# A streaming encoder layer on one core: the states of its state space groups keep the rows of the turning frame, and first operands of its MLP are formed on VectorE

## The chip, the core and the metric

The kernel runs on one of the eight cores of a Trainium2 chip. Its engines work side by side, each through its own queue in order: TensorE (PE: matmuls, with weight loads as PEld), VectorE (DVE), ScalarE (ACT), GpSimd (POOL) and SyncE (SP, which here issues DMAs). They wait for each other on semaphores. The metric is the device time of one execution in microseconds (us).

## The reference

One layer over 16 meta tokens, 2048 prompt frames and 64 frames of a running stream, 2128 tokens of width 1024, all in float32. Cut to what matters here:

```python
z = rmsnorm(h, norm1_g) @ w_in                # split into q, k, v (attention) and u
q, k, v, u = split(z)                         # u: 32 groups of 16 channels
attn = sliding-window attention with sinks
bu = einsum(u, B_bar)                         # per group: 64 complex states
xs = scan(x[t] = a * x[t-1] + bu[t])          # complex, diagonal; the sample starts from h0
y  = Re(C x) + D u                            # back to 16 channels per group
zs = gelu(y); s = zs * sigmoid(zs @ w_glu + b_glu)
h  = h + concat(rmsnorm(attn), rmsnorm(s)) @ w_out
f  = rmsnorm(h, norm2_g) @ w_up               # 1024 -> 4096
return h + square(relu(f)) @ w_down, ..., xs[last] of both streams
```

## The kernel before

**Layout and stages.** Activations lie with channels on the partitions and tokens along the row. Matmuls split each float32 operand into a high part in float32r (a rounded copy made on ACT) and a low part, the rest (a subtraction on DVE or POOL, names ending in `l`), and sum three products; so each product on PE has a cast on ACT and a subtraction on DVE behind it. Some small matmuls run on plain float32: one such matmul of the program is two PE records in the profile. The stages follow each other: projection to u, projection to q, k, v with attention (to some 450 us), the state space groups together with the attention half of the output projection (to some 600 us), the GLU with the other half of that projection (to some 770 us), and the MLP.

**State space groups.** Tokens are taken in blocks of 8, 266 blocks. The 32 groups run as 16 pairs. For a pair `j`, `ssm_in` multiplies u with a table from `reca` into two PSUM banks, `pss`, one per group: the 64 real parts in rows 0 to 63, the 64 imaginary parts in rows 64 to 127. `ssm_align` (ACT, four copies of 64 rows) turns this around into `RI`: real parts of both groups in one half of the row, imaginary parts in the other, group 0 in rows 0 to 63 and group 1 in rows 64 to 127. `ssm_mix` works in this arrangement on DVE: steps 0 and 1 turn the values into a rotating frame (`o1`, `o2`, `ab`), in which the complex scan becomes two real ones (steps 2 and 3, L1272, one long call for the prompt and one of 8 columns for the sample each); step 4 multiplies back (`p1`, `p2`, L1276 and L1277), and step 5 forms the states `H` (two tiles that take turns). There, four calls of 64 rows (L1282 and L1285) put each group's states in a tile with real parts in rows 0 to 63 and imaginary parts in rows 64 to 127, two small copies keep the final states (`fin`, L1287) and put the sample's start in its place (L1288, from `h0`). `ssm_out` sums, per group, a product over u (L1294) and one over the 128 rows of states (L1295) with tables from `recb` into `psy`; `ssm_done` copies it out on ACT as `ys`, `ssm_write` stores it. `store_k` has written these tables, four pairs at a time.

**Opening of the MLP.** The MLP uses Strassen's scheme on halves of tokens, inputs and hidden units: seven products of half size instead of eight, each over sums or differences of blocks of the normed activations. `x0_load` reads blocks a, b, c of the first tokens from `hd`, where the output projection has stored them; `gain` multiplies by the weight of the norm on ACT (L1778, with `slow`) and the reciprocal root on POOL (L1782), or both on DVE (L1780); `x0_sub` (L1809) forms the differences, `x_cut` (L1790 and L1791) the high and low parts `xh`, `xl`. Block d needs the output projection's last store, so `x0_last` loads it last, in two parts `sa`, `sb`, and `x0_rest` treats it. `product(i, q)` are the matmuls (L1973) into banks bA, bB, bC. `h_squares` adds up the squares of the output projection for the norm (L1648, L1651), on POOL.

**What sets the order.** The program text is not the order. `Order.arrange` takes all instructions, a cost for each, their dependencies and buffers, runs a list schedule backward and forward, and fixes the order on each engine. So each edit can move instructions elsewhere. It knows that POOL and DVE calls that read two operands from SBUF exclude each other (`ported`). POOL calls stand in the same plan as all others.

Of the kernel before, what the change touches and what calls it, by code (L numbers as in the profile page):

```python
# [377 lines left out]
def tile_trunk(ctx: ExitStack, tc: tile.TileContext, I, O, dbg=None, stop=None):  # L378
# [60 lines left out]
    def prep(pp, pg, pgb):  # L439
# [185 lines left out]
        def store_k(q, pk):  # L625
# [3 lines left out]
            for c, t in enumerate((vr, vi)):  # L629
                for gg in range(2):  # L630
                    r = slice(64 * gg, 64 * gg + 64)
                    nc.sync.dma_start(recb[js, 64 * c : 64 * c + 64, gg * P : (gg + 1) * P].rearrange("j p (d c) -> p j d c", c=16),
                                      t[r, :, 1:9, :])
# [585 lines left out]
    def ssm_open():  # L1219
        Sx["sp"] = ssp.enter_context(pool("sp", 1, "right"))  # L1220
        h0 = Sx["h0"] = Sx["sp"].tile([P, G], F32, name="h0")
        nc.sync.dma_start(h0, I["h0"])
        Sx["fin"] = Sx["sp"].tile([P, 2, G], F32, name="fin")
# [32 lines left out]
    def ssm_mix(j, i):  # L1256
# [21 lines left out]
        elif i == 5:  # L1278
            H = x["H"] = GH[j % 2]
            for gg in range(2):  # L1280
                r = slice(64 * gg, 64 * gg + 64)
                v.tensor_sub(H[0:64, gg, 1:], x["p1"][r, 0], x["p2"][r, 1])  # L1282
            for gg in range(2):
                r = slice(64 * gg, 64 * gg + 64)
                v.tensor_add(H[64:, gg, 1:], x["p1"][r, 1], x["p2"][r, 0])  # L1285
            gs = slice(2 * j, 2 * j + 2)
            v.tensor_copy(Sx["fin"][:, :, gs].rearrange("p q g -> p g q"), H[:, :, PCH : NCH + 1 : NCH - PCH])  # L1287
            v.tensor_copy(H[:, :, PCH], Sx["h0"][:, gs])  # L1288

    def ssm_out(j):  # L1290
        x = Sx[j]
        y = x["y"] = Sx["py"]()
        for gg in range(2):
            nc.tensor.matmul(y[:, gg, :NCH], x["rb"][:, (2 + gg) * P : (3 + gg) * P], x["U"][:, gg], start=True, stop=False)  # L1294
            nc.tensor.matmul(y[:, gg, :NCH], x["rb"][:, gg * P : gg * P + P], x["H"][:, gg, 0:NCH], start=False, stop=True)  # L1295

# [329 lines left out]
    nc.sync.dma_start(O["st"], Sx["fin"])  # L1626
# [13 lines left out]
    def h_squares(n, e, x):  # L1640
# [5 lines left out]
        if e == 0:  # L1646
            HS[n] = WO["na"].tile([P, OB], F32, tag=f"hs{n}", name="hs", bufs=1)
            nc.gpsimd.tensor_add(HS[n], sq[:, 0], sq[:, 1])  # L1648
        else:
            for i in range(2):  # L1650
                nc.gpsimd.tensor_add(HS[n], HS[n], sq[:, i])  # L1651
# [121 lines left out]
    def gain(x, k0, nh, slow=False):  # L1773
# [7 lines left out]
        if slow:  # L1781
            nc.gpsimd.tensor_mul(x, x, M["rs"][:, nh].unsqueeze(1).broadcast_to((P, 2, OB)))  # L1782
# [327 lines left out]
    def rs_first(nh):  # L2110
# [6 lines left out]
    out_block(NOB - 1, {0: (lambda: x0_sub("d", "b", "a", e), lambda: u_get(0, (0, 0), (1, 0))),  # L2117
                        1: (lambda: x0_cut(1, "a", v), lambda: x0_gain("c", 1, 1), lambda: u_get(0, (1, 1), (0, 1))),
                        2: (lambda: x0_sub("b", "c", "b", e),), 3: (lambda: x0_sub("a", "c", "d", v),),
# [140 lines left out]
```

## Time and profile before

| | us |
|---|---|
| median of 3 runs (2100.11 to 2104.24) | 2102.73 |
| the profiled execution, its own time | 2103.09 |
| its span in the profile | 2100.5 |
| PE busy, 12100 matmul records | 2003.0 (95%) |
| PEld busy | 1931.1 (92%) |
| DVE busy | 1800.0 (86%) |
| ACT busy | 1221.7 (58%) |
| POOL busy | 397.0 (19%) |

The span is what the profile's rows lie in; 2.6 us of the execution's time lie around it. Busy shares are means over stages with different limits, and so say little alone. In the trace, `<-` names what ended a wait; a name such as `xl` stands for all buffers of that name, and `L1791` is the kernel's line. A row with `128x266 f32<-128x266 f32` gives rows by columns of the output and the input; `128*128` on PE gives rows and columns of the weights.

### The profile page before, as it was taken

What the parts mean: (1) busy time and instruction counts of PE and PEld (TensorE: products, weight loads), DVE (VectorE), ACT (ScalarE), POOL (GpSimd) and SP (SyncE); (2) the same over time, 40 slices, a digit from 0 to 9 for tenths busy, and PEclk for the clock granted to TensorE, in tenths of its full rate; (3) what the DMA queues carried; (4) which work ended last, traced back from release to release, by engine and by line L of the source; (5) the groups of instructions that cost most, each with busy time, mean ns of one, the idle gap of its engine ahead of it and who ended that gap; (6) DMA issues with size and microseconds to landing.
All of it is one profiled execution on the core that took longest, in us unless ns stands there. A gap on an engine that the chain in (4) does not pass through costs nothing.

```text
span 2100.5 us, 34600 instructions
## 1 busy us (share of the span) xinstructions
PE 2003.0 (95%) x12100; PEld 1931.1 (92%) x12100; DVE 1800.0 (86%) x3315; ACT 1221.7 (58%) x2496; POOL 397.0 (19%) x525
## 2 busy tenths in 40 slices
PE   8989999997789988999999999999999999999999
PEld 8987888786679977999999999999999999999999
DVE  8958996679977778999999998789978977887778
ACT  6447677743255545655555666665656655566554
POOL 7954311000002052333233301000000100000000
PEclk9999999999899998999999999999999999999999
DMA  6532332467664385654666676556745764444432
GB/s 224 153 63 76 98 97 72 146 210 239 205 209 127 118 263 189 212 181 165 226 215 201 210 249 220 160 150 207 224 140 152 240 200 141 137 135 138 138 121 96
DMA packets 308335, 354.41 MB, mean 169 GB/s; under 512 B 28865, under 2 KB 220992, under 8 KB 307650
## 3 DMA queue, kind: packets, MB, share of 16 engines
q1 hardware_dynamic: 308018, 352.21, 53.8%
q8 instruction: 95, 1.56, 0.3%
q14 instruction: 78, 0.64, 0.1%
q10 hardware_dynamic: 144, 0.00, 0.0%
HBM read 260.15 MB, written 94.07 MB: 169 GB/s over the span
## 4 chain that ended last, share of the span: by engine, by line
PE 67%; DVE 19%; ACT 5%; DMA 5%; issue 3%; SPq 0%; POOL 0%; DVEq 0%; ACTq 0%; POOLq 0%
PE psd L2068 28%; PE bB L1973 10%; PE bA L1973 10%; PE bC L1973 8%; PE pso L1454 3%; PE psqkv L920 3%; PE psg L1672 2%; DMA hd<-xo 1%; PE pu L825 1%; DVE ul L1963 1%; DVE ab L1272 1%; DVE ss L799 1%; PE pv L1185 1%; DVE wl L2037 1%; DVE acc L2077 1%
## 5 line engine op out<-in xcount | busy, mean ns | idle before, releaser
L2068 PE MATMUL psd<-hh,wh 128*128 128x352 f32 x1344 | 433.8, 323 | 3.8 <-DVE acc L2077 2.9
L2068 PE MATMUL psd<-hl,wh 128*128 128x352 f32 x1344 | 432.0, 321 | 2.0 <-DVE hl L2056 2.0
L2068 PE MATMUL psd<-hh,wl 128*128 128x352 f32 x1344 | 430.6, 321 | 0.0
L2077 DVE TENSOR_TENSOR acc<-psd,acc 128x352 f32<-128x352 f32 x624 | 313.2, 514 | 36.5 <-PE psd L2068 35.7
L2068 PEld LDWEIGHTS psd<-hh,wh 128*128 128x128 f32 x1344 | 252.0, 188 | 6.2 <-DVE acc L2077 3.8
L2068 PEld LDWEIGHTS psd<-hl,wh 128*128 128x128 f32 x1344 | 252.7, 188 | 2.7 <-DVE hl L2056 2.6
L2068 PEld LDWEIGHTS psd<-hh,wl 128*128 128x128 f32 x1344 | 252.3, 188 | 0.0
L1962 ACT CAST uh<-ur 128x512 fp32r<-128x512 f32 x144 | 89.3, 620 | 151.3 <-PE bB L1973 64.0
L2037 DVE TENSOR_TENSOR wl<-d,wh 128x512 fp32r<-128x512 f32 x240 | 175.2, 730 | 0.3 <-ACT wh L2036 0.2
L2036 ACT CAST wh<-d 128x512 fp32r<-128x512 f32 x240 | 146.5, 617 | 34.1 <-PE psd L2068 28.3
L1973 PE MATMUL bA<-xl,uh 128*128 128x352 f32 x480 | 155.9, 325 | 5.4 <-DVE xl L1791 5.4
L1973 PE MATMUL bA<-xh,uh 128*128 128x352 f32 x480 | 157.6, 328 | 3.0 <-ACT xh L1790 1.6
L1962 ACT CAST uh<-us 128x512 fp32r<-128x512 f32 x128 | 79.4, 621 | 133.5 <-PE bB L1973 68.5
L1973 PE MATMUL bB<-xh,uh 128*128 128x352 f32 x480 | 156.0, 325 | 0.0
L1973 PE MATMUL bA<-xh,ul 128*128 128x352 f32 x480 | 155.9, 325 | 0.0
L1973 PE MATMUL bB<-xh,ul 128*128 128x352 f32 x480 | 155.4, 324 | 0.0
L1973 PE MATMUL bB<-xl,uh 128*128 128x352 f32 x480 | 154.8, 323 | 0.0
L920 PE MATMUL psqkv<-wqa,xh 128*128 128x384 f32 (+1 forms) x544 | 138.3, 348 | 7.0 <-ACT z L933 6.7
L1973 PE MATMUL bC<-xl,uh 128*128 128x352 f32 x384 | 125.4, 327 | 5.6 <-DVE xl L1791 5.6
L2056 DVE TENSOR_TENSOR hl<-hid,hh 128x352 fp32r<-128x352 f32 x240 | 129.2, 538 | 1.1 <-ACT hh L2055 1.1
L1963 DVE TENSOR_TENSOR ul<-ur,uh 128x512 fp32r<-128x512 f32 x144 | 108.7, 755 | 24.6 <-ACT uh L1962 24.6
L1973 PE MATMUL bC<-xh,ul 128*128 128x352 f32 x384 | 125.2, 326 | 2.3 <-DVE ul L1963 2.2
(446 smaller groups left out, 5295.7 us busy)
## 6 DMA issues: line engine op xcount, KB each, us to landing
ur<-in_w_up_dram SPq DMA_DIRECT2D x160, 256.0 KB
d<-in_w_down_dram SPq DMA_DIRECT2D x128, 256.0 KB
us<-usd SPq DMA_DIRECT2D x128, 256.0 KB
d<-dsd SPq DMA_DIRECT2D x96, 256.0 KB
hd<-xo SPq DMA_DIRECT2D x48, 352.0 KB
usd<-s SPq DMA_DIRECT2D x64, 256.0 KB
dsd<-d SPq DMA_DIRECT2D x48, 256.0 KB
dx<-in_w_down_dram SPq DMA_DIRECT2D x48, 256.0 KB
```

The lines of the kernel that those rows point to most:

```text
L799: nc.vector.tensor_reduce(out=ss[b], in_=x.rearrange("p k n -> p n k"), axis=AX.X, op=ALU.add)
L920: nc.tensor.matmul(t["ps"][c][:n, :384], x, w[k][:, c * 384 : c * 384 + 384], start=(k == 0 and i == 0), stop=(k == KT - 1 and i == 2))
L1454: nc.tensor.matmul(ps, w, x, start=(i == 0), stop=(i == len(seq) - 1))
L1672: nc.tensor.matmul(ps, w[:, k, m * P : (m + 1) * P], x[:, k], start=(k == 0 and i == 0), stop=(k == 3 and i == 2))
L1962: nc.scalar.copy(h, src)
L1963: nc.vector.tensor_sub(l, src, f32(h))
L1973: nc.tensor.matmul(ps, w[:, k], x[:, k], start=(p in BANK and k == 0 and a == 0), stop=False, skip_group_check=True)
L2036: nc.scalar.copy(h, src)
L2037: (e if p in POOLED[i >= NPR] else v).tensor_sub(l, src, f32(h))
L2056: eng.tensor_sub(l, src, f32(h))
L2068: nc.tensor.matmul(ps, w[:, c], y, start=(p in DFIRST and n == 0), stop=False, skip_group_check=True)
L2077: v.tensor_add(ACC[eh, nh][:, x], ps, ACC[eh, nh][:, x])
```

## The change

It has two parts. In the state space groups, `H` keeps the arrangement of the rotating frame: group 0 in rows 0 to 63, group 1 in rows 64 to 127, real and imaginary parts side by side along the row. Two DVE calls of 128 rows (L1279, L1280 in the new numbering) replace the four of 64. `ssm_out` takes two products of 64 rows per group instead of one of 128 (L1298), `store_k` stores the tables accordingly, with two DMAs instead of four. The two small copies per pair go from DVE to ACT (L1281, L1282); `h0` comes from the input `par`, which has it in this arrangement, and a new function `ssm_last` turns the final states into the output's arrangement with four copies on ACT. In the other part, calls go from POOL to DVE: the sums of squares of `h_squares`, the product with the root in `gain`, two differences of `x0_sub` and the low part of `x0_cut(2, ...)`.

```diff
@@ store_k
             for c, t in enumerate((vr, vi)):
-                for gg in range(2):
-                    r = slice(64 * gg, 64 * gg + 64)
-                    nc.sync.dma_start(recb[js, 64 * c : 64 * c + 64, gg * P : (gg + 1) * P].rearrange("j p (d c) -> p j d c", c=16),
-                                      t[r, :, 1:9, :])
+                nc.sync.dma_start(recb[js, :, c * P : (c + 1) * P].rearrange("j p (d c) -> p j d c", c=16), t[:, :, 1:9, :])
@@ ssm_open
-        h0 = Sx["h0"] = Sx["sp"].tile([P, G], F32, name="h0")
-        nc.sync.dma_start(h0, I["h0"])
-        Sx["fin"] = Sx["sp"].tile([P, 2, G], F32, name="fin")
+        h0 = Sx["h0"] = Sx["sp"].tile([P, 2, PAIRS], F32, name="h0")
+        nc.sync.dma_start(h0, I["par"][:, 3:5])
+        Sx["fin"] = Sx["sp"].tile([P, 2, 2, PAIRS], F32, name="fin")
+        Sx["st"] = Sx["sp"].tile([P, 2, G], F32, name="st")
@@ ssm_mix, step 5
             H = x["H"] = GH[j % 2]
-            for gg in range(2):
-                r = slice(64 * gg, 64 * gg + 64)
-                v.tensor_sub(H[0:64, gg, 1:], x["p1"][r, 0], x["p2"][r, 1])
-            for gg in range(2):
-                r = slice(64 * gg, 64 * gg + 64)
-                v.tensor_add(H[64:, gg, 1:], x["p1"][r, 1], x["p2"][r, 0])
-            gs = slice(2 * j, 2 * j + 2)
-            v.tensor_copy(Sx["fin"][:, :, gs].rearrange("p q g -> p g q"), H[:, :, PCH : NCH + 1 : NCH - PCH])
-            v.tensor_copy(H[:, :, PCH], Sx["h0"][:, gs])
+            v.tensor_sub(H[:, 0, 1:], x["p1"][:, 0], x["p2"][:, 1])
+            v.tensor_add(H[:, 1, 1:], x["p1"][:, 1], x["p2"][:, 0])
+            nc.scalar.copy(Sx["fin"][:, :, :, j].rearrange("p q c -> p c q"), H[:, :, PCH : NCH + 1 : NCH - PCH])
+            nc.scalar.copy(H[:, :, PCH], Sx["h0"][:, :, j])
+
+    def ssm_last():
+        for c in range(2):
+            for gg in range(2):
+                nc.scalar.copy(Sx["st"][64 * c : 64 * c + 64, :, gg::2], Sx["fin"][64 * gg : 64 * gg + 64, :, c])
+        nc.sync.dma_start(O["st"], Sx["st"])
@@ ssm_out
-            nc.tensor.matmul(y[:, gg, :NCH], x["rb"][:, gg * P : gg * P + P], x["H"][:, gg, 0:NCH], start=False, stop=True)
+            r = slice(64 * gg, 64 * gg + 64)
+            for c in range(2):
+                nc.tensor.matmul(y[:, gg, :NCH], x["rb"][r, c * P : c * P + P], x["H"][r, c, 0:NCH], start=False, stop=(c == 1))
@@ after the last pair
-    nc.sync.dma_start(O["st"], Sx["fin"])
+    ssm_last()
@@ h_squares
-            nc.gpsimd.tensor_add(HS[n], sq[:, 0], sq[:, 1])
+            nc.vector.tensor_add(HS[n], sq[:, 0], sq[:, 1])
-                nc.gpsimd.tensor_add(HS[n], HS[n], sq[:, i])
+                nc.vector.tensor_add(HS[n], HS[n], sq[:, i])
@@ gain
-            nc.gpsimd.tensor_mul(x, x, M["rs"][:, nh].unsqueeze(1).broadcast_to((P, 2, OB)))
+            nc.vector.tensor_mul(x, x, M["rs"][:, nh].unsqueeze(1).broadcast_to((P, 2, OB)))
@@ the last output block, and x0_rest
-    x0_sub("d", "b", "a", e)
+    x0_sub("d", "b", "a", v)
-    x0_sub("b", "c", "b", e)
+    x0_sub("b", "c", "b", v)
-    x0_cut(2, "d", e)
+    x0_cut(2, "d", v)
```

The order of the instructions is unchanged up to some 450 us of the trace before, and again from some 1050 us on. Between them it moves at these places.

DVE in the state space stage, one pair, before: `H` with a number is one of the two state tiles, `ab` the scan's values, `xo` an addition of the output projection.

```order
L1282 TENSOR_TENSOR H_5195<-p_5885,p_5886 64x266 x2
L1285 TENSOR_TENSOR H_5195<-p_5885,p_5886 64x266 x2
L1272 SCALAR_TENSOR_TENSOR ab<-r_90,ab 128x258
L1287 COPY fin<-H_5195 128x2x2
L1272 SCALAR_TENSOR_TENSOR ab<-r_90,g_89,ab 128x8
L1288 COPY H_5195<-h_5190 128x2
L1272 SCALAR_TENSOR_TENSOR ab<-r_90,ab 128x258
L1272 SCALAR_TENSOR_TENSOR ab<-r_90,g_89,ab 128x8
L1496 TENSOR_TENSOR xo<-pso,xo 128x352 x2
```

The same place after the change:

```order
L1266 TENSOR_TENSOR ab<-o_5873,o_5874 128x266
L1270 SCALAR_TENSOR_TENSOR ab<-r_90,ab 128x258
L1270 SCALAR_TENSOR_TENSOR ab<-r_90,g_89,ab 128x8
L1279 TENSOR_TENSOR H_5188<-p_5878,p_5879 128x266
L1280 TENSOR_TENSOR H_5188<-p_5878,p_5879 128x266
L1270 SCALAR_TENSOR_TENSOR ab<-r_90,ab 128x258
L1270 SCALAR_TENSOR_TENSOR ab<-r_90,g_89,ab 128x8
L1499 TENSOR_TENSOR xo<-pso,xo 128x352 x2
```

The four calls of 64 rows have become two of 128, and stand between the scans of the next pair; the two copies are gone from this engine.

PE in the same stage, before: `psy<-U` and `psy<-H` are the products over u and over the states, `pss` the way into the states of a later pair, `pso` the output projection.

```order
L1294 MATMUL psy<-U,rb 128x266
L1295 MATMUL psy<-H_5193,rb 128x266
L1294 MATMUL psy<-U,rb 128x266
L1295 MATMUL psy<-H_5193,rb 128x266
L1245 MATMUL pss<-U,ra 128x266 x2
L1294 MATMUL psy<-U,rb 128x266
L1454 MATMUL pso<-xh,zt 128x352
```

After the change:

```order
L1295 MATMUL psy<-U,rb 128x266
L1298 MATMUL psy<-H_5186,rb 128x266 x2
L1295 MATMUL psy<-U,rb 128x266
L1298 MATMUL psy<-H_5186,rb 128x266 x2
L1243 MATMUL pss<-U,ra 128x266 x2
L1295 MATMUL psy<-U,rb 128x266
L1298 MATMUL psy<-H_5188,rb 128x266 x2
L1295 MATMUL psy<-U,rb 128x266
L1298 MATMUL psy<-H_5188,rb 128x266 x2
```

Each product over the states has become two, one behind the other; PE's other rows are the same number, 278 matmuls of the output projection in this stage in both kernels, spread differently.

DVE at the opening of the MLP, before: from the last addition of the output projection (`xo<-pso`) on; `xa` to `xd` are blocks, `sa` and `sb` the parts of the block loaded last, `xl` low parts of the products' operands, `ul` that of a weight.

```order
L1496 TENSOR_TENSOR xo<-pso,xo 128x352
L1809 TENSOR_TENSOR xa<-xc,xd 128x704
L1791 TENSOR_TENSOR xl_8176<-xd,xh_8175 128x704
L1809 TENSOR_TENSOR xa<-xc,xd 128x704
L1791 TENSOR_TENSOR xl_8106<-xa,xh_8105 128x704
L1780 SCALAR_TENSOR_TENSOR sa<-sa,g_7792,rs 128x352 x2
L1791 TENSOR_TENSOR xl_8176<-xd,xh_8175 128x704
L1791 TENSOR_TENSOR xl_8106<-xa,xh_8105 128x704
L1780 SCALAR_TENSOR_TENSOR sb<-sb,g_7792,rs 128x352 x2
L1791 TENSOR_TENSOR xl_8220<-xc,xh_8219 128x704
L1809 TENSOR_TENSOR xa<-sa,xa 128x704
L1791 TENSOR_TENSOR xl_8220<-xc,xh_8219 128x704
```

After the change, from the two last additions of the output projection on:

```order
L1966 TENSOR_TENSOR ul<-s,uh 128x512
L1499 TENSOR_TENSOR xo<-pso,xo 128x352 x2
L1794 TENSOR_TENSOR xl_8103<-xa,xh_8102 128x704 x2
L1794 TENSOR_TENSOR xl_8173<-xd,xh_8172 128x704
L1794 TENSOR_TENSOR xl_8188<-xb,xh_8187 128x704
L1794 TENSOR_TENSOR xl_8173<-xd,xh_8172 128x704
L1794 TENSOR_TENSOR xl_8217<-xc,xh_8216 128x704
L1794 TENSOR_TENSOR xl_8188<-xb,xh_8187 128x704
L1794 TENSOR_TENSOR xl_8217<-xc,xh_8216 128x704
L1966 TENSOR_TENSOR ul<-s,uh 128x512
L1783 SCALAR_TENSOR_TENSOR sa<-sa,g_7789,rs 128x352 x2
L1966 TENSOR_TENSOR ul<-ur,uh 128x512
```

All low parts of the blocks a to d stand ahead of the two products of `sa` and `sb`; before, four of the rows shown stand behind the products of `sa`, those of `xb` come later still, and POOL had the differences `xd` and `xb`. On PE the first product's twelve matmuls have moved in among the last of the output projection.

## Rows read from the trace of the kernel before

**Rows 1.** Busy time by stage: us, busy us of each engine (instructions), clock, DMA share.
```profile
458.90:594.00 135.10, 103.68 (x466) 84.59 (x465) 133.02 (x310) 43.59 (x92) 0.00 (x0) 0.91 0.72 229
...
640.00:754.00 114.00, 113.44 (x691) 111.09 (x689) 86.08 (x138) 60.56 (x101) 21.35 (x18) 1.00 0.50 153
754.00:769.00 15.00, 14.94 (x91) 14.60 (x92) 9.85 (x14) 4.62 (x8) 13.13 (x8) 1.00 0.89 292
769.00:831.00 62.00, 45.69 (x218) 40.76 (x217) 50.81 (x65) 32.44 (x62) 22.94 (x13) 0.81 0.57 190
840.00:1260.00 420.00, 414.22 (x2564) 411.01 (x2563) 412.10 (x738) 252.99 (x516) 124.69 (x71) 1.00 0.64 207
```

**Rows 2.** Groups of 458.9 to 594 us: count | busy us, mean ns | idle before.
```profile
L1295 PE MATMUL psy<-H,rb 128*128 128x266 f32 x64 | 22.7, 440 | 8.9 <-DVE H L1288 8.9
L1254 ACT COPY RI<-pss 64x266 f32<-64x266 f32 x60 | 22.5, 376 | 35.5 <-PE pss L1245 30.9 <-DVE ab L1267 4.0
...
L1245 PE MATMUL pss<-U,ra 128*128 128x266 f32 x60 | 19.4, 442 | 14.2 <-DMA ra<-reca 12.4 <-DMA U<-ud 1.7 <-issue 0.2
...
L1282 DVE TENSOR_TENSOR H<-p,p 64x266 f32<-64x266 f32 x32 | 13.6, 424 | 0.6 <-PE psy L1295 0.4
```

**Rows 3.** DVE in order of time, one pair of groups: start us, us, instruction.
```profile
502.06 0.42 DVE L1268 TENSOR_TENSOR ab<-o,o 128x266 f32<-128x266 f32 x1
502.40 0.86 DVE L1282 TENSOR_TENSOR H<-p,p 64x266 f32<-64x266 f32 x2
503.28 0.88 DVE L1285 TENSOR_TENSOR H<-p,p 64x266 f32<-64x266 f32 x2
504.19 0.70 DVE L1272 TENSOR_TENSOR_SCAN ab<-r,ab 128x258 f32<-128x258 f32 x1
504.80 0.15 DVE L1287 COPY fin<-H 128x4 f32<-128x4 f32 x1
504.86 0.23 DVE L1272 TENSOR_TENSOR_SCAN ab<-r,g,ab 128x8 f32<-128x8 f32 x1
```

**Rows 4.** PE in order of time, state space stage.
```profile
491.71 0.61 PE L1295 MATMUL psy<-H,rb 128*128 128x266 f32 x2
492.16 0.39 PE L1245 MATMUL pss<-U,ra 128*128 128x266 f32 x1
```

**Rows 5.** Groups of PE over the span, products of 64 and 81 rows.
```profile
L1185 PE MATMUL pv<-e,VB 81*128 81x256 f32 x132 | 40.4, 389 | 0.7 <-ACT e L1176 0.7
...
L1185 PE MATMUL pv<-e,VB 64*128 64x256 f32 x4 | 1.4, 428 | 0.0
```

**Rows 6.** PE's weight loads in order of time, near the 64-row product.
```profile
177.36 0.29 PEld L1185 LDWEIGHTS pv<-e,VB 64*128 64x128 f32 x2 [0.16 <-issue]
```

**Rows 7.** Groups of POOL from 640 to 786 us.
```profile
L1651 POOL TENSOR_TENSOR hs<-hs,sq 128x352 f32<-128x352 f32 x12 | 13.6, 1135 | 14.2 <-ACT sq L1645 13.7
...
L1809 POOL TENSOR_TENSOR xd<-xb,xa 128x704 f32<-128x704 f32 x2 | 4.0, 2023 | 0.0
```

**Rows 8.** DVE in order of time at the opening of the MLP.
```profile
769.21 0.51 DVE L1496 TENSOR_TENSOR xo<-pso,xo 128x352 f32<-128x352 f32 x1
...
771.54 2.35 DVE L1791 TENSOR_TENSOR xl<-xd,xh 128x704 fp32r<-128x704 f32 x1
...
774.62 0.88 DVE L1791 TENSOR_TENSOR xl<-xa,xh 128x704 fp32r<-128x704 f32 x1
775.42 1.07 DVE L1780 SCALAR_TENSOR_TENSOR sa<-sa,g,rs 128x352 f32<-128x352 f32 x2
...
780.24 1.92 DVE L1780 SCALAR_TENSOR_TENSOR sb<-sb,g,rs 128x352 f32<-128x352 f32 x2 [2.15 <-DMA d<-in_w_down_dram]
```

**Rows 9.** PE in order of time at the opening of the MLP.
```profile
783.01 0.66 PE L1973 MATMUL bC<-xl,uh 128*128 128x352 f32 x1 [2.63 <-DVE xl L1791]
...
800.81 0.66 PE L1973 MATMUL bA<-xl,uh 128*128 128x352 f32 x1 [3.31 <-DVE xl L1791]
```

More of the change, by code (lines that the diff above doesn't have):

```diff
@@ L2116, in tile_trunk @@
                         5: (lambda: rs_first(1), lambda: x0_load("c", 1, 1)), 6: (lambda: x0_gain("a", 0, 0),), 7: (lambda: x0_gain("b", 0, 1),)})
-    out_block(NOB - 1, {0: (lambda: x0_sub("d", "b", "a", e), lambda: u_get(0, (0, 0), (1, 0))),
+    out_block(NOB - 1, {0: (lambda: x0_sub("d", "b", "a", v), lambda: u_get(0, (0, 0), (1, 0))),
                         1: (lambda: x0_cut(1, "a", v), lambda: x0_gain("c", 1, 1), lambda: u_get(0, (1, 1), (0, 1))),
-                        2: (lambda: x0_sub("b", "c", "b", e),), 3: (lambda: x0_sub("a", "c", "d", v),),
+                        2: (lambda: x0_sub("b", "c", "b", v),), 3: (lambda: x0_sub("a", "c", "d", v),),
                         4: (lambda: u_sum(0, 1, 2),), 5: (lambda: x0_cut(6, "a", v),),
```

## The prediction

> **What bounds the kernel now.** I read the view by stages first: busy time of each engine, granted clock and DMA share per stretch [rows 1]. The reader is to see that the limits differ. From 640 to 754 us PE is busy 113.44 of 114 us, and from 840 to 1260 us 414.22 of 420: there PE sets the pace, at 414.22 / 2564 = 0.162 us a record. In between lie two stretches where PE is held. One is the state space stage, 458.9 to 594 us: DVE is busy 133.02 of 135.1 us, PE has 466 records. The other is the opening of the MLP, 769 to 831 us: 218 PE records in 62 us, which at 0.162 us would be 35.3 us, so 26.7 us are lost, at a mean granted clock of 0.81. After 840 us the order of the instructions is nearly the same in both kernels, and PE sets the pace, so time won in these two stretches should stay won.
>
> Next I read the costliest groups inside the state space stage [rows 2] and one pair of groups on DVE in order of time [rows 3]; then PE [rows 4, 5, 6]; last POOL, DVE and PE around the opening of the MLP [rows 7, 8, 9].
>
> **State space stage, DVE.** Before, the states of a pair are written by four calls of 64 rows, 32 calls each of L1282 and L1285, 0.424 us each [rows 2]. From start to start the four take 504.19 - 502.40 = 1.79 us [rows 3]. After, two calls of 128 rows and the same 266 columns do it. A call of that very size (L1268) stands 502.40 - 502.06 = 0.34 us before the next [rows 3]; the calls that go took 0.45. So two cost 0.68 to 0.90 us, and a pair saves 0.89 to 1.11 us; 16 pairs save 14.2 to 17.8 us. I take the lower figure, since the new calls read what was just written, as the old ones do. The two small copies per pair leave DVE too: the next call starts 504.86 - 504.80 = 0.06 us after one [rows 3], so 32 of them give 1.9 us. DVE's need falls by 16.1 us, to 135.1 - 16.1 = 119 us.
>
> **The copies on ACT.** ACT is busy 43.59 of 135.1 us in the stage [rows 1]. Before shows no ACT copy of 4 elements: one costs above nothing and below the 0.376 us of the 64x266 copy [rows 2]; I take 0.15, what the same copy lasts on DVE [rows 3]. 32 are 5 us, hidden by ACT's idle time. They add a wait: PE's product of the states now waits for ACT, whose queue also holds the copies out of PSUM (RI, ys). Behind a waiting fin copy stand the RI copies of a pair that DVE takes up about one pair later, so a wait of a microsecond or two hides there. Today the two copies stand among the scans, the first 504.80 - 504.19 = 0.61 us after the last H call gave way to a scan; two copies of 0.15 us on ACT end no later. I cost it at nothing; without that cover it is 32 times 0.15, 5 us.
>
> **The products on PE.** Before, each group takes one product of 128 rows over the states; after, two of 64 rows: 32 more. One program product is two records, and takes 492.16 - 491.71 = 0.45 us from start to start at full clock [rows 4]. No row shows a 64-row product of this kind. Below it could be near nothing, if halves ran side by side; but both halves of a group use the same rows and follow each other, so nothing suggests it. Above, the nearest pair: the 64*128 products of the attention last 428 ns against 389 ns for 81*128 [rows 5], a tenth more. I take 0.45: 14.4 us more. PE's need today at full clock: 188 fp32 records (64 over the states, 64 over U into the same sums, 60 into the states) at 0.225 us, 270 others at 0.162 and 8 of the norm sums (counted like them) give 42.3 + 45.0 = 87 us of 135.1 [rows 1, 2]; after, 102 us. The mean clock of 0.91 can add up to 0.09 x 135.1 = 12 us. That is still under DVE's 119 us, but close enough that waits of both engines on each other show. I allow 4 us: the stage then lasts 123 us, 12 us less. Bounds: 19 us less (all DVE gains, no coupling) and 3 us less (PE at 114 and each DMA wait of today's 14.2 us on PE [rows 2] also held by the denser DVE).
>
> The Trainium skill, TensorEngine Tiling (Array Packing), section Key Properties, says that a change of the tiling mode drains TensorE. Were a 64-row product such a mode, each pair would change it four times.
>
> The weight load ahead of the only 64-row product of the attention stands 0.16 us idle [rows 6]; 64 such gaps are 10.2 us, PE's need 112 us. This is a rival below.
>
> **Stores and loads.** The 64-row halves of recb are stored by two DMAs instead of four for each of four quarters, the same bytes; the load of rb is unchanged in size. h0 comes from another input with the same 16 KB. The final states take four ACT copies of 64x32 more before their store; nothing on the chain waits for that store, and ACT is idle there. Together nothing (0 to 1 us, if the last ys copy stands behind them).
>
> **Sums of squares on DVE.** 14 calls of 1.135 us leave POOL [rows 7]. On DVE a call of 704 columns takes 0.80 us [rows 8], so these of 352 cost less than 11 us in all, in a stretch where DVE is busy 86.08 of 114 us and PE full [rows 1]. PE hides it; 0 to 1 us.
>
> **The opening of the MLP.** Twelve calls of 128x704 (products with the norm, differences, two low parts) leave POOL, where one takes 2.02 us [rows 7], for DVE, where the next starts 775.42 - 774.62 = 0.80 us later [rows 8]. DVE's own calls beside them were stretched: the same low part takes 2.35 us at 771.54 and 0.88 us at 774.62 [rows 8], and POOL is busy 13.13 of the 15 us before 769 [rows 1]. So the chain of ten calls halves, and DVE as a whole is hardly fuller: 9.6 us come, some 9 us of stretch go. The order then changes in a way that matters more. Before, the low parts of xc and xb stood behind the two sb products, which waited for a load until 780.24 [rows 8]; PE stood 2.63 us at 783.01 and 3.31 us at 800.81 for them [rows 9]. After, all eight low parts stand ahead of that load, so the first product's twelve matmuls run between the output projection's, and four more products follow on. These two stalls go (5.9 us). Of the low clock, 0.19 x 62 = 11.8 us are at stake [rows 1]; I take back a quarter, 3 us, since after these products PE must still wait for the sa and sb loads, which follow the last store (769.21 to 780.24, 11 us [rows 8]). Against it, DVE must do the ten calls before its last xo additions: 8 us into a stretch with 5 us idle plus the stretch that goes [rows 1]; 1 us late. Sum: 8 us less. Bounds: 0 (the load's 11 us set it all) and 16 (26.7 less those 11).
>
> **Sum.** The profiled run took 2103.09 us; 2103.1 - 12 - 8 = 2083. The median of the runs is 2102.73, 0.4 us less, so this stands for either.
>
> **Rivals.**
> - *PE becomes the limit of the state space stage, and the kernel is slower.* PE's other work there is 87 - 14.4 = 73 us. To be 4 us slower with the opening's 8 us gained, the stage must last 147 us, so a 64-row product must cost (147 - 73) / 64 = 1.16 us instead of 0.45. At 1.3 us the stage lasts 156, the kernel 2116. For it: the clock already dips (0.91 mean [rows 1]), and it would dip more where products are slow to start. Against: 428 against 389 ns [rows 5]. Chance 0.06.
> - *DMA keeps the stage long.* DMA share is 0.72 of 135.1 us, 97 us of transfers [rows 1], and PE already waits 14.2 us for ra and U [rows 2]. Denser work may turn these into waits of DVE: a stage of 131 us, 2103 - 4 - 8 = 2091. Chance 0.14.
> - *Draining between full and half products*, the rule above: 10 us more of PE need, beside DVE's 119; the stage gains 8 instead of 12: 2087. The 0.16 us row could as well be a late semaphore. Chance 0.12.
> - *The opening hangs on the load alone*: POOL was slow beside a wait that stays. Gain 1 there: 2103 - 12 - 1 = 2090. For it: the 11 us from last store to sb. Chance 0.15.
> - *The change doesn't do what it says*: the wide call costs twice the half one. L1268 excludes it nearly (0.34 us for 128 rows) [rows 3]; 2103 - 2 - 8 = 2093. Chance 0.03.
> - The forecast, 2083: 0.50.
>
> **How the numbers follow.** The best bounds together give 2103 - 19 - 16 = 2068; the worst of the forecast and of two mild rivals at once, 2103 - 3 - 1 = 2099. I give 2068 to 2099. What is left out above is the first rival and some unnamed cost of the dense stage. A difference under 0.2% (4.2 us) can't be told from none here: faster 0.90, the same 0.04, slower 0.06.
>
> **What would show it.** In the profile after: the stage from the first o1 call to the last psy product lasts 119 to 127 us with DVE still over 90% busy; L1279 and L1280 32 calls in all, at most 0.45 us apart; twice as many psy records over the states, at 0.22 us spacing; no DVE call of 128x704 of 2 us between 754 and 785; the stalls of PE on xl after the first load gone, one wait for the sa and sb blocks in their place. I am wrong if DVE in the stage is well under 90% busy with PE full (first or third rival), if DVE idles on RI behind ra loads (second), or if the stretch from the last pso product to steady PE is still about 60 us (fourth).

## The result, and the profile after

| | before | after |
|---|---|---|
| median, us (runs) | 2103.48 (2100.11 to 2105.42, 4) | 2075.00 (2072.99 to 2080.32, 4) |
| ratio, 95% interval | | 0.987 (0.9857 to 0.9884) |
| span of the profiled execution, us | 2100.5 | 2072.7 |

The changed kernel is 28 us faster; forecast were 20 (2083, from 2068 to 2099). The span is 27.8 us shorter. First the view by stages after, with the columns of [rows 1]: the state space stage from the start of its first `o1` call to the start of its last `psy` record, a piece of the GLU stage, the opening of the MLP, and steady MLP.

```profile
456.80:573.88 117.08, 114.96 (x527) 86.77 (x527) 115.36 (x248) 51.49 (x129) 0.00 (x0) 1.00 0.83 268
620.00:734.00 114.00, 113.27 (x689) 110.94 (x688) 88.22 (x153) 62.33 (x106) 2.58 (x2) 1.00 0.49 152
753.40:815.40 62.00, 51.87 (x282) 48.90 (x282) 53.34 (x83) 36.26 (x70) 21.32 (x10) 0.92 0.73 236
815.00:1235.00 420.00, 412.07 (x2565) 409.43 (x2564) 413.27 (x740) 252.65 (x515) 122.72 (x71) 1.00 0.64 207
```

Between the same two events before:

```profile
458.88:593.48 134.60, 103.18 (x463) 84.14 (x463) 133.04 (x310) 43.10 (x90) 0.00 (x0) 0.91 0.72 229
```

So the stage is 17.5 us shorter, and DVE's busy time in it falls by 17.7. DVE is idle 1.7 us of it, about as before (1.6). PE, which had 463 records, has 527, and is now busy 114.96 of 117.08 us; its mean granted clock rose from 0.91 to 1.00. In the 62 us of the opening PE does 282 records instead of 218: 62 - 282 x 0.162 = 16.3 us lost instead of 26.7 [rows 1], 10.4 less. The GLU stage and the steady MLP are much as before: 0.7 and 7.9 us without PE, before 0.6 and 5.8 [rows 1].

The span's 27.8 us in order of time: the stage began 2.1 us earlier (456.80 after 458.88) and is 17.5 shorter; from its end to the last product of the output projection it is 4.2 us more (753.24 - 573.88 after 768.59 - 593.48), 1.9 of them 12 products of the MLP that now stand ahead of that last one; and from there to the end 12.4 less. A second profile of the same changed kernel, on another chip, has the stage at 117.03 us but starts it 5.6 us later than this one, so a start that moves by some microseconds is no effect of the change.

One of DVE's two calls of states and one of ACT's two copies, in the form of [rows 2]; their partners L1280 and L1282 are alike:

```profile
L1279 DVE TENSOR_TENSOR H<-p,p 128x266 f32<-128x266 f32 x16 | 6.9, 429 | 0.0
L1281 ACT COPY fin<-H 128x4 f32<-128x4 f32 x16 | 3.2, 198 | 15.4 <-DVE H L1280 15.3
```

And one pair of groups in order of time, to set beside [rows 3]:

```profile
518.69 0.43 DVE L1279 TENSOR_TENSOR H<-p,p 128x266 f32<-128x266 f32 x1
519.03 0.43 DVE L1280 TENSOR_TENSOR H<-p,p 128x266 f32<-128x266 f32 x1
519.37 0.69 DVE L1270 TENSOR_TENSOR_SCAN ab<-r,ab 128x258 f32<-128x258 f32 x1
```

Two calls of 128 rows stand 0.34 us apart, and what follows starts 0.68 us after the first; four of 64 took 1.79 [rows 3]. A pair saves 1.11 us, 16 pairs 17.8. The two copies last 0.20 us on ACT.

PE in order of time, the products of one group:

```profile
519.79 0.61 PE L1243 MATMUL pss<-U,ra 128*128 128x266 f32 x2
520.33 1.16 PE L1298 MATMUL psy<-H,rb 64*128 64x266 f32 x4
521.42 0.72 PE L1295 MATMUL psy<-U,rb 128*128 128x266 f32 x2
521.98 0.61 PE L1243 MATMUL pss<-U,ra 128*128 128x266 f32 x2
```

Four records over `H` (two products of 64 rows) and then a change back to 128 rows take 521.42 - 520.33 = 1.09 us, where four records at 0.225 would take 0.90; from `pss` to the products over `H` it is 0.54 instead of 0.45. Here and below, 0.225 us is half of the 0.45 that a product of two records took in [rows 4].

The opening of the MLP. DVE's low parts of 128x704 stand 0.80 us apart, and none lasts 2 us; all eight low parts of `xa` to `xd` are made before `sa` and `sb`, the parts of the block loaded last, are used:

```profile
755.64 0.88 DVE L1794 TENSOR_TENSOR xl<-xd,xh 128x704 fp32r<-128x704 f32 x1
756.44 0.88 DVE L1794 TENSOR_TENSOR xl<-xb,xh 128x704 fp32r<-128x704 f32 x1
...
764.80 1.08 DVE L1783 SCALAR_TENSOR_TENSOR sb<-sb,g,rs 128x352 f32<-128x352 f32 x2 [0.92 <-DMA d<-in_w_down_dram]
```

What PE waited for between 753 and 830 us (us in all, times, longest):

```profile
PE bC L1976 <- ACT uh L1965: 5.0, 1, 5.0
PE bC L1976 <- DVE xl L1794: 3.1, 2, 2.7
```

The stalls of [rows 9] on `xl` after the load (2.63 and 3.31 us) are gone; one of 2.7 us stands at the very start. In their place comes something that I had not foreseen: one wait of 5.0 us for a cast `uh` of a weight sum on ACT.

### The profile page after: what moved, and what is told of

Same layout as the page of the kernel before. It is cut to its first block, busy times and chain, and to the rows that moved or that the text cites. A ratio compares the mean times of both kernels' runs of the same rounds, so it can differ in the third digit from the quotient of the medians.

```text
span 2072.7 us, 34670 instructions
## 1 busy us (share of the span) xinstructions
PE 2008.1 (97%) x12164; PEld 1929.7 (93%) x12164; DVE 1787.0 (86%) x3277; ACT 1227.3 (59%) x2532; POOL 361.4 (17%) x499
## 4 chain that ended last, share of the span: by engine, by line
PE 51%; DVE 2%; DMA 0%; issue 0%; SPq 0%; DVEq 0%
PE psd L2071 26%; PE bA L1976 9%; PE bB L1976 9%; PE bC L1976 7%; DVE acc L2080 0%; DVE wl L2040 0%; DVE hl L2059 0%; DVE ul L1966 0%; DMA usd<-s 0%; DVE d L2023 0%; DMA dsd<-d 0%; DVE hid L1994 0%; DVE bt L2047 0%; DVE xl L1794 0%; DVE d L2025 0%
## 5 line engine op out<-in xcount | busy, mean ns | idle before, releaser
L1976 PE MATMUL bC<-xh,uh 128*128 128x352 f32 x384 | 125.1, 326 | 5.0 <-ACT uh L1965 5.0
```

What stands on the lines that cost most here:

```text
L1976: nc.tensor.matmul(ps, w[:, k], x[:, k], start=(p in BANK and k == 0 and a == 0), stop=False, skip_group_check=True)
```

## The experiments

Times are medians of 4 to 10 runs a kernel; ratios are to the kernel before, measured on the same chip at the same time.

| kernel | us | ratio (95% interval) | stage, us | DVE / PE busy in it | mean granted clock |
|---|---|---|---|---|---|
| before, as profiled at first | 2103.48 | 1 | 134.60 | 133.04 / 103.18 | 0.91 |
| changed, once more | 2079.64 | 0.9876 (0.9860 to 0.9892) | 117.03 | 115.36 / 115.53 | 1.00 |
| state space part alone | 2085.86 | 0.9903 (0.9885 to 0.9921) | 117.02 | 115.34 / 114.90 | 1.00 |
| MLP part alone | 2099.96 | 0.9970 (0.9957 to 0.9982) | 134.51 | 133.05 / 105.41 | 0.91 |
| four calls of 64 rows | 2097.97 | 0.9963 (0.9951 to 0.9975) | 135.48 | 131.81 / 123.30 | 0.96 |
| products padded to 128 rows | 2076.90 | 0.9865 (0.9848 to 0.9881) | 117.24 | 114.64 / 107.72 | 0.99 |
| products over U first | 2081.82 | 0.9885 (0.9867 to 0.9903) | 117.26 | 113.59 / 101.96 | 0.97 |
| groups alternating | 2081.74 | 0.9882 (0.9865 to 0.9898) | 118.75 | 113.63 / 101.68 | 0.96 |
| changed, without `o2` | 2076.66 | 0.9851 (0.9824 to 0.9877) | 113.85 | 106.31 / 113.14 | 1.00 |
| alternating, without `o2` | 2075.64 | 0.9849 (0.9827 to 0.9872) | 110.36 | 105.73 / 100.71 | 0.95 |
| three sums on DVE | 2071.60 | 0.9834 (0.9816 to 0.9852) | 119.59 | 115.43 / 117.39 | 0.99 |
| one sum on DVE | 2075.16 | 0.9845 (0.9819 to 0.9870) | 116.81 | 115.35 / 114.73 | 1.00 |
| padded, and three sums | 2072.50 | 0.9838 (0.9813 to 0.9863) | 117.17 | 114.70 / 107.67 | 0.99 |

The stage is taken from the start of the first `o1` call to the start of the last `psy` record in each profile. The kernel before took 2106.99 us beside the parts alone, U first and alternating, 2104.86 beside the changed kernel once more, the four calls, the padded products and the three sums, and 2104.73 beside the rest; kernels that ran beside different ones are compared by ratio.

**Each part alone.** The first takes the MLP's edits back, the second makes them alone in the kernel before.

```diff
 # state space part alone: back to POOL, six places such as
-            nc.vector.tensor_add(HS[n], sq[:, 0], sq[:, 1])
+            nc.gpsimd.tensor_add(HS[n], sq[:, 0], sq[:, 1])
...
-            x0_cut(2, "d", v)
+            x0_cut(2, "d", e)
```

> The state space part alone; the calls of the MLP's opening and the squares are back on POOL. Theory A (both parts gain, each in its own stretch, and the gains add): the state stage ends as early as in the changed kernel, the opening is back to about 62 us from the last output projection to steady PE: 2083 to 2085 us, some 9 above the changed kernel. Rival (the opening hangs on the load of the last block alone, and the shorter rest came from the state stage): within 2 us of the changed kernel, 2073 to 2077.

> The calls from POOL to DVE alone; the state space groups as before. Theory A: the state stage lasts 135 us again, the opening gains 8 to 10 us: 2093 to 2096 us. Rival (nothing from the opening): 2102 to 2104.

The parts add: 0.97% and 0.30%, against 1.3% together. The MLP part gives 6.3 us, less than the 8 to 10 expected. Without the MLP's edits the opening keeps its old stall, here 3.50 us (before 3.31 [rows 9]); with them alone in the kernel before, the new wait for `uh` is there as well:

```profile
785.21 0.66 PE L1976 MATMUL bA<-xl,uh 128*128 128x352 f32 x1 [3.50 <-DVE xl L1794]
```

```profile
806.62 0.66 PE L1973 MATMUL bC<-xh,uh 128*128 128x352 f32 x1 [5.05 <-ACT uh L1962]
```

**Is it the number of DVE calls?** The places of the rows stay as changed, and with them the 64-row products and the copies on ACT; only the calls are cut in two again.

```diff
-            v.tensor_sub(H[:, 0, 1:], x["p1"][:, 0], x["p2"][:, 1])
+            for gg in range(2):
+                r = slice(64 * gg, 64 * gg + 64)
+                v.tensor_sub(H[r, 0, 1:], x["p1"][r, 0], x["p2"][r, 1])
 # and the same for tensor_add
```

> The changed kernel as it is, on the chip of the three kernels sent with it, so that they are set against it directly. Its ratio to the kernel before was 0.987 (0.9857 to 0.9884). All theories: 0.986 to 0.989 again; the state space stage from its first product to its last 64-row product 107 us, one wait of TensorE of 5.0 us at the third bC of the MLP's opening.

> The changed kernel, but the turned-back states H are made by four VectorE calls of 64 rows a pair of groups instead of two of 128 rows; places of the rows, products and everything else stay as changed. Theory A (VectorE paces the state space stage, and only its busy time counts): 32 more calls of some 0.44 us, 14 us longer than the changed kernel, ratio to it 1.0067 (1.005 to 1.0085), with TensorE's clock in the stage still above 0.95. Rival B (TensorE with its 64-row products and their changes of mode paces the stage; TensorE was busy 115.5 of 117.6 us): within 3 us of the changed kernel. Rival C (the gain is in TensorE's clock and its waits, which the layout of the rows set free): 3 to 8 us longer, the clock staying at 1.00 and VectorE idle in part.

```profile
458.78:594.26 135.48, 123.30 (x529) 88.70 (x528) 131.81 (x280) 51.83 (x129) 0.00 (x0) 0.96 0.72 233
```

```profile
503.91 0.88 DVE L1281 TENSOR_TENSOR H<-p,p 64x266 f32<-64x266 f32 x2
504.80 0.90 DVE L1284 TENSOR_TENSOR H<-p,p 64x266 f32<-64x266 f32 x2
505.72 0.70 DVE L1270 TENSOR_TENSOR_SCAN ab<-r,ab 128x258 f32<-128x258 f32 x1
```

The time goes up by 2097.97 - 2079.64 = 18.3 us, and the stage is 135.48 us, a little longer than before the change (134.60). From the first half call to the scan it is 505.72 - 503.91 = 1.81 us instead of 0.68: 16 x 1.13 = 18.1 us. So the number of calls accounts for the whole gain of the stage; Theory A holds, though I had expected 14, and its clock above 0.95 as well: 0.96. Rival B falls: PE has the same products, DVE alone changed. Rival C falls too: it had 3 to 8 us and a clock that stays at 1.00. The copies on ACT show no gain of their own here: without them on DVE it is 1.2 us less busy than before, and 2.1 more idle.

**What do the 64-row products cost PE?** First without any: the tables of the other group are padded with zeros, so that every product has 128 rows. The tables are one and a half times as wide.

```diff
+            RBT[i] = Sx["sp"].tile([P, 6 * P], F32, name=f"rb{i}")
+            nc.gpsimd.memset(RBT[i][64:, 0 : 2 * P], 0.0)
+            nc.gpsimd.memset(RBT[i][0:64, 2 * P : 4 * P], 0.0)
...
-                nc.tensor.matmul(y[:, gg, :NCH], x["rb"][r, c * P : c * P + P], x["H"][r, c, 0:NCH], start=False, stop=(c == 1))
+                k = (2 * gg + c) * P
+                nc.tensor.matmul(y[:, gg, :NCH], x["rb"][:, k : k + P], x["H"][:, c, 0:NCH], start=False, stop=(c == 1))
```

> The changed kernel, but the products over the states take all 128 rows: the records' rows of the other group hold zeros (three standing tiles, zeroed once, and three loads a pair of groups instead of one), so that no product of 64 rows is left and TensorE never changes between whole and half arrays. Same number of products and the same VectorE work. Theory A (VectorE paces the stage; the 64 changes of about 0.2 us, 13 us of TensorE, lie beside it): within 3 us of the changed kernel, ratio 0.9985 to 1.0015. Rival B (TensorE paces): 8 to 13 us shorter, ratio 0.994 to 0.996. Rival D (two half-array products side by side save more than the changes cost, so that whole-array products make TensorE the limit): 5 to 15 us longer, waits of VectorE for psum tiles or of the stage for TensorE.

```profile
458.36:575.60 117.24, 107.72 (x531) 92.39 (x531) 114.64 (x247) 50.13 (x129) 0.00 (x0) 0.99 0.86 266
```

The products of one group in the changed kernel, then of the same group padded:

```profile
530.95 0.61 PE L1295 MATMUL psy<-U,rb 128*128 128x266 f32 x2
531.50 1.16 PE L1298 MATMUL psy<-H,rb 64*128 64x266 f32 x4
532.59 0.71 PE L1295 MATMUL psy<-U,rb 128*128 128x266 f32 x2
```

```profile
531.12 0.61 PE L1302 MATMUL psy<-U,rb 128*128 128x266 f32 x2
531.56 1.06 PE L1305 MATMUL psy<-H,rb 128*128 128x266 f32 x4
532.47 0.61 PE L1302 MATMUL psy<-U,rb 128*128 128x266 f32 x2
```

From one product over U to the next it is 532.47 - 531.12 = 1.35 us; in the changed kernel 532.59 - 530.95 = 1.64. So a group's two changes cost 0.29 us here, and 32 groups would cost 9.3; PE's busy time in the stage fell by 115.53 - 107.72 = 7.8, with the same number of records. The stage did not get shorter (117.24 against 117.03), and the total lies 2.7 us lower, inside both intervals. The changes of mode are there, and DVE hides them: Theory A.

Then with fewer changes: both products over U ahead of all four over `H`; in a second version the four alternate between rows 0 to 63 and 64 to 127.

```diff
         for gg in range(2):
             nc.tensor.matmul(y[:, gg, :NCH], x["rb"][:, (2 + gg) * P : (3 + gg) * P], x["U"][:, gg], start=True, stop=False)
-            r = slice(64 * gg, 64 * gg + 64)
-            for c in range(2):
+        for c in range(2):
+            for gg in range(2):
+                r = slice(64 * gg, 64 * gg + 64)
                 nc.tensor.matmul(y[:, gg, :NCH], x["rb"][r, c * P : c * P + P], x["H"][r, c, 0:NCH], start=False, stop=(c == 1))
```

> The changed kernel, but the two products over u of a pair stand first and the four 64-row products after them: two changes between 128-row and 64-row products per pair instead of four. If each change costs PE 0.2 us (as the gaps after the change read), PE needs 32 x 0.2 = 6.4 us less in the state stage. Theory A (DVE paces that stage): the total stays within 2 us of the changed kernel, 2073 to 2077, and the gaps are half as many in the trace. Rival B (PE, busy 115.48 of 117.6 us there, has become the pace): 4 to 6 us less, 2069 to 2071.

> As the kernel with the products over u first, but the four 64-row products alternate between the two groups, rows 0 to 63 and rows 64 to 127. If products on different rows run side by side, two take the time of one (0.45 us instead of 0.90), 16 x 0.9 = 14 us less of PE. Theory A: the total stays at 2073 to 2077 whatever PE gains. Rival B (PE paces the stage): without running side by side 2069 to 2071, with it 2063 to 2067. If they do not run side by side, the spacing of the records stays 0.22 us.

The first rows are of the first version, the view of the stage is of the second:

```profile
521.68 1.06 PE L1295 MATMUL psy<-U,rb 128*128 128x266 f32 x4
522.67 1.18 PE L1299 MATMUL psy<-H,rb 64*128 64x266 f32 x8
523.78 0.71 PE L1243 MATMUL pss<-U,ra 128*128 128x266 f32 x2
```

```profile
458.54:577.29 118.75, 101.68 (x521) 79.80 (x521) 113.63 (x244) 49.01 (x126) 0.00 (x0) 0.96 0.80 260
```

Eight records over `H` take 523.78 - 522.67 = 1.11 us, with the change back, where eight at 0.225 would take 1.80: products on the two halves of the rows ran side by side. These are of the first version, whose text does not alternate; a record does not say which half it uses, so the order in PE's queue is not shown. PE's busy time falls by 14 us. The stage does not: 117.26 and 118.75 us. Again DVE paces it. The times, 2082 us, lie above the 2073 to 2077 expected, but by ratio (0.9885 and 0.9882) both are as the changed kernel (0.987 and 0.9876). But look at the clock: with more idle time PE is granted a mean of 0.97 and 0.96 of full speed here, not 1.00, and in the second version DVE, busy 113.63 of 118.75 us, stands idle 5.1 us instead of 1.7. What PE saves comes back in part as waits.

**What would be late next?** A product of the stage is left out, the second of the turn into the frame (`o2`; `o1` stands in its place, so the results of that part differ): 11.3 us less for DVE.

```diff
+            x["o2"] = x["o1"]
             v.tensor_mul(x["o1"], x["RI"], tc_)
-            v.tensor_mul(x["o2"], x["RI"], ts_)
```

> The changed kernel without the product o2 of the turn into the frame: one VectorE call of 128x532 (0.705 us) a pair of groups is left out, 16 in all, 11.3 us of VectorE, and o1 stands in its place in what follows, so the state space part computes something else. Everything on TensorE, ScalarE and the queues is as in the changed kernel. Theory A2 (VectorE paces the stage, and TensorE, busy 98.4 of every 100 us with 64-row products and their changes of mode, lies right behind it): the stage 2 to 4 us shorter, not 11, and VectorE now waits for TensorE; ratio to the kernel before 0.986 to 0.987, where the changed kernel has 0.9876. Rival E (only VectorE counts, TensorE has room): the stage 9 to 12 us shorter, ratio 0.982 to 0.984.

> The same product o2 left out, in the version in which the products of the two groups are issued alternately after both products over U: there TensorE was busy 84.3 of 100 us in the stage, and the time was that of the changed kernel (ratio 0.9882). Theory A2: with room on TensorE the 11.3 us of VectorE come off in great part, the stage 7 to 11 us shorter than that version's, ratio 0.983 to 0.985; e10 and e11 differ by 4 to 8 us. Rival E: 9 to 12 us in both, no difference between them. Rival F (something else, the loads of DMA or ScalarE's copies, is the limit by then): within 3 us of that version in both.

```profile
459.34:573.19 113.85, 113.14 (x522) 85.55 (x522) 106.31 (x234) 52.04 (x130) 0.00 (x0) 1.00 0.85 279
```

```profile
463.63:573.99 110.36, 100.71 (x518) 78.91 (x517) 105.73 (x231) 51.17 (x129) 0.00 (x0) 0.95 0.86 282
```

In the changed kernel 11.3 us less of DVE work shorten the stage by 3.2 (117.03 to 113.85), and PE is then busy 113.14 us of it: PE is the limit there. With the alternating products it is 8.4 (118.75 to 110.36). For the stage A2 holds, and E and F fall. The totals do not show the difference between the two that I expected (2076.66 and 2075.64; the second began its stage 4.3 us later), so by the total this stays undecided.

**The new wait in the opening.** The changed kernel's engines in order of time. First POOL:

```profile
761.29 1.52 POOL L1945 TENSOR_TENSOR s<-s,ur 128x512 f32<-128x512 f32 x1 [7.43 <-DVE ul L1966]
775.51 9.57 POOL L1949 TENSOR_TENSOR s<-ur,s 128x512 f32<-128x512 f32 x1 [12.70 <-DVE ul L1966]
```

The sum before took 1.52 us, this one 9.57. On DVE, calls with two inputs follow each other without a gap from 765.79 to 783.96 us, and the sum ends, at 785.08, 1.1 us after the last of them:

```profile
765.79 0.89 DVE L1794 TENSOR_TENSOR xl<-sa,xh 128x704 fp32r<-128x704 f32 x1
...
783.28 0.68 DVE L2040 TENSOR_TENSOR wl<-d,wh 128x512 fp32r<-128x512 f32 x1
```

Then ACT and PE:

```profile
781.92 0.62 ACT L2039 CAST wh<-dx 128x512 fp32r<-128x512 f32 x1 [1.79 <-DVE dx L2030]
782.44 0.61 ACT L2039 CAST wh<-d 128x512 fp32r<-128x512 f32 x1
785.12 0.62 ACT L1965 CAST uh<-s 128x512 fp32r<-128x512 f32 x1 [2.06 <-POOL s L1949]
```

```profile
785.79 0.66 PE L1976 MATMUL bC<-xh,uh 128*128 128x352 f32 x1 [5.01 <-ACT uh L1965]
```

So I took the sum to be the cause, and moved the three sums of that tile to DVE.

```diff
             SW[w] = SW[2] if w == 4 else u_tile("s", "s")
+            e = nc.vector if i == 1 else nc.gpsimd      # the other version: if (i, w) == (1, 4)
```

> The changed kernel, but the three sums of weight blocks for the second tile of the MLP (and of it alone) are made on VectorE instead of GpSimd, among them the one that took 9.57 us on GpSimd beside a run of VectorE calls and that TensorE waited 5.01 us for. Theory A (GpSimd's sum was starved by the VectorE calls beside it, and that wait is a loss of the changed kernel): the 5.0 us wait is gone, VectorE has some 2 to 4 us more to do in the opening, the time 2 to 5 us shorter than the changed kernel, ratio 0.9975 to 0.999. Rival B (VectorE is the limit of the opening in any case): the wait comes back at an xl or uh of the opening, and the time is within 1.5 us of the changed kernel or longer.

> The changed kernel with one call moved: the last sum of the second MLP tile, which took 9.57 us on GpSimd, goes to VectorE; the tile's two other sums stay on GpSimd. If the loss is that one starved call, TensorE's wait of 5.0 us is gone and the time is 4 to 8 us below the changed kernel, as with all three moved (ratio to the kernel before 0.9834 to 0.9855). If it is the load of GpSimd in the opening that counts, or the other two sums are starved in its place, a wait of 3 to 5 us comes back at another uh, and the time is within 2 us of the changed kernel.

The longest waits of PE in the opening, of the version with three sums and of that with one:

```profile
PE bB L1977 <- DVE xl L1794: 3.3, 1, 3.3
```

```profile
PE bB L1977 <- ACT uh L1966: 2.2, 1, 2.2
```

With three sums on DVE the median lies 8.0 us below the changed kernel's, measured on the same chip at the same time, where 2 to 5 were expected. With one it lies 4.5 us below the same run, but level with the changed kernel's first (2075.00); the changed kernel was not run beside it and the intervals overlap, so its gain is not shown. The wait of 5.0 us is gone in both. Others came in its place, though. The first 100 us of the opening, of the changed kernel (once more) and of the version with three sums:

```profile
756.50:856.50 100.00, 89.47 (x525) 86.73 (x524) 90.45 (x145) 62.53 (x123) 38.57 (x23) 0.95 0.72 228
756.03:856.03 100.00, 89.30 (x521) 87.08 (x520) 93.33 (x148) 60.07 (x121) 27.26 (x19) 0.94 0.71 230
```

PE does no more records there. After 62 us it was ahead (317 records instead of 287), then lost that lead in further waits. So the 8.0 us are measured, but in these profiles they are not won in the opening, and where they come from is not shown.

Nor was the wait itself the work of the held sum alone. The MLP part alone, above, has the same wait of 5.05 us, and there POOL's sum was not held up so long:

```profile
796.30 2.71 POOL L1946 TENSOR_TENSOR s<-ur,s 128x512 f32<-128x512 f32 x1 [12.64 <-DVE ul L1963]
```

```profile
797.96 1.60 DVE L2022 TENSOR_TENSOR d<-d,d 128x512 f32<-128x512 f32 x1
799.48 1.78 DVE L2024 TENSOR_TENSOR d<-d,d 128x512 f32<-128x512 f32 x1
```

```profile
802.50 0.62 ACT L2036 CAST wh<-dx 128x512 fp32r<-128x512 f32 x1 [2.36 <-DVE dx L2027]
804.91 0.62 ACT L2036 CAST wh<-dx 128x512 fp32r<-128x512 f32 x1 [1.79 <-DVE dx L2027]
805.95 1.14 ACT L1962 CAST uh<-s 128x512 fp32r<-128x512 f32 x2
```

Here two POOL calls got in between, this one and the next, and two DVE calls of 0.68 us took 1.60 and 1.78. The cast `uh` ran 6.9 us after the sum was done (805.95 after 799.01): it stood on ACT behind three casts `wh`, two of which waited for `dx` of DVE. In the changed kernel the same casts ended at 783.05, and the sum held `uh` only for the last 2.06 us. With three sums on DVE the order is new, too: there `uh` stands ahead of the `wh` casts that wait for `dx`. With one, the `uh` of the remaining 2.2 us still stands behind them. So two things end within 2 us of each other, and by this reading the order of ACT's queue accounts for the larger part of the wait. A version that changes this order alone was not run, so that is argued, not shown.

**The two together.** Padded products and three sums on DVE, no further edit:

> The two edits that came out below the changed kernel together: products over the states padded to 128 rows (2.7 us below it) and the three weight sums of the second MLP tile on VectorE (8.0 us below it). If the gains are of different places and add: 9 to 12 us below the changed kernel, ratio to the kernel before 0.982 to 0.984. Otherwise no better than the sums alone, 0.9834.

2072.50 us, ratio 0.9838: no better than the sums alone, as the second case of the expectation has it. So the padding's 2.7 us can't be told from noise. Three sums on DVE has the lowest median of all, 2071.60, 0.39% below the changed kernel beside it.

## Why the prediction was right or wrong

*Direction, place and range* were right. DVE paced the stage before and after; PE did not become the limit.

*The stage's term was too small: 12 us instead of 17.5;* the stage lasts 117.1 us, just below the 119 to 127 that were named as the sign. Two steps made it so. "I take the lower figure, since the new calls read what was just written, as the old ones do": the spacing is 0.34 us as in [rows 3], not 0.45, and the calls save 17.8 us instead of 14.2. The half calls with the new rows are at 0.45 again, so it goes with the number of rows, not with what was written last. And "I allow 4 us" for waits of both engines on each other: by the spacings DVE gives up 17.8 + 1.9 = 19.7 us, so about 2 us did not come off. They are not those waits, for DVE idles 1.7 us, as before; two more helper calls of DVE (L419 and L420) fall into the stage, about 1 us, and the rest is not traced. The low clock of before (0.91), counted as a load on PE, did not stay: it belonged to a PE that stood idle 31 us. In the changed stage PE stood idle 2.1 us in all, and its mean clock was 1.00. The versions that give PE room lie between, at 0.95 to 0.99 in the table. The stage's lower bound, 3 us less, does not follow from its own terms (114 + 14.2 = 128 us is 7 less); it only widened the range.

*Products of 64 rows.* "I take 0.45: 14.4 us more" holds for two that follow each other with the same rows, but for the changes: 0.90 of the 1.09 us for four records. Side by side was possible only between the groups, and there it happened once their products stood together.

*Draining as a rival.* The Trainium skill, TensorEngine Tiling (Array Packing), section Key Properties, says that a change of tiling mode drains TensorE, and that tiles can run in parallel. The trace agrees with both: 0.29 us for the two changes of a group, 7.8 us of PE in the stage, and eight half-height records in 1.11 us. The rival's price of 10 us was about right. What failed in it is the 4 us it took from the stage: DVE hides all of it, and only with 11 us less of DVE work do PE's needs, these changes among them, decide (113.85 against 110.36 us).

*DMA as a rival.* PE's waits for `ra` and `U`, 14.2 us before [rows 2], did not turn into waits of DVE, though the mean DMA share rose from 0.72 to 0.83. They shrank instead:

```profile
L1243 PE MATMUL pss<-U,ra 128*128 128x266 f32 x60 | 17.1, 396 | 0.3 <-DMA ra<-reca 0.3
```

*The copies on ACT* cost 0.20 us each, estimated at 0.15. PE waits 1.8 us in all for them, hidden by DVE. They were not tried by themselves.

*Sums of squares on DVE*, at nothing: PE loses 0.73 of 114 us in the GLU stage, 0.56 before [rows 1].

*The opening: 8 us forecast.* The MLP part alone gives 0.30% (0.18 to 0.43), 6.3 us, and the lost PE time of the window fell by 10.4. The two stalls went as said. That it hung on the load alone is wrong. Instead of the one wait for `sa` and `sb` that was to be left, there is the new wait of 5.0 us for `uh`: with the calls from POOL, DVE's queue became dense, and I looked only at what leaves POOL, not at the sums that stay there, nor at what ACT's queue holds behind DVE's results.

## What to carry to other kernels

Read the cost of a call from start to start in a full stretch, for the same number of rows: two of 128 rows took 0.68 us where four of 64 took 1.81, and the whole gain of the stage lay there. When a paced stage has a second engine that fills up, its extra work can be free up to that point, and taking it away again brings nothing; leaving work out on either engine shows how far. When a wait has a named releaser, look at what else stands on that engine's queue just ahead, and for a second kernel in which the named cause is missing but the wait is there. When a wait is gone, count the records over a longer stretch: the time may be lost again behind it.

## What the runs showed of the hardware

- DVE calls of 64 rows did not overlap: 0.45 us each from start to start, longer than each lasts (0.43 us), with or without a shift between row halves. Those of 128 rows and the same 266 columns stood 0.34 us apart.
- Going from 128-row to 64-row products and back cost PE 0.29 us where one group is set beside the same group padded, and 7.8 us of busy time over 32 groups; eight records on rows 0 to 63 and 64 to 127 took 1.11 us, less than eight in turn (1.80).
- A run of two-input DVE calls without a gap held a two-input POOL call for 9.57 us, until the run ended. The Trainium skill, SBUF — State Buffer, section Who interferes with whom, says that a DVE instruction with two SBUF inputs contends with a GpSimd instruction that reads SBUF, and that issue order decides who blocks. The trace agrees that one of the two waits, and goes further: POOL waited for a whole run of calls, not for one. In another run two POOL calls came in between, and two DVE calls took 1.60 and 1.78 us instead of 0.68.
- The same stage ran at a mean granted clock of 1.00 where PE did more for the same result (115.0 us busy), and of 0.96 where it did less (101.7).
